# Sums of x in eight small pieces with buffers of their own, a ring for weights alone, and the last values placed behind the last scan step

## The chip, the cores and the metric

One core of a Trainium2 chip runs the whole kernel. The metric is device time in microseconds (us), the median over runs of the same program; lower is better. The engines are TensorE (PE: matmuls and transposes; PEld is its weight load), VectorE (DVE), ScalarE (ACT), GpSimd (POOL) and SyncE (SP), which here issues most of the DMAs in one queue.

## The reference

One layer of a hybrid encoder block on 1024 positions, with 16 learned meta tokens in front (T = 1040), d = 1024, all in float32. Cut to what matters:

```python
u = _rms_norm(h, pre_w)
z = u @ w_in                    # 1024 x 7680, one combined projection
rq, rk, rv, rg, aq, ak, av, ag, gr, ga = _split_in(z)

# branch A: retention, 4 heads, keys 128 wide, values 256 wide, chunks of 128,
# one scan forward and one backward, summed; then a norm per head
o_r = _bidirectional_retention(rq, rk, rv, lg_f, lg_b)[:, META_PAD:]
o_r = ((o_r - mu) * lax.rsqrt(var + EPS)).reshape(B, T, RET_V)
o_r = o_r * ret_nw * jax.nn.silu(rg)
y_r = o_r @ w_rb

# branch B: attention in a window of +-128, 8 heads in 2 groups, meta keys and a sink
o_a = _windowed_sink_attention(aq, ak, av, sink)[:, META_PAD:].reshape(B, T, ATT_Q)
y_a = (o_a * jax.nn.silu(ag)) @ w_ab

mix = jax.nn.sigmoid(gr) * y_r + jax.nn.sigmoid(ga) * y_a
return h + _rms_norm(mix @ w_o, post_w)
```

## The kernel before

**Matmuls.** A float32 product is made of three passes in a faster format (fp32r): each operand is split into a high part, cast by ScalarE or GpSimd, and a low part, which VectorE gets as the difference (the helper `dve_lo`, line 89). `mm3` then issues high by high, high by low and low by high, which are lines 73, 74 and 75 in the profile. In the names an `h` or `l` at the end tells the part: `wh` and `wl` are the halves of a weight tile `wr`, `weh` and `wel` those of `we`, `aqh` and `aql` those of `aq`, `kTh` and `kTl` those of the keys.

**Stages.** About 0 to 40 us: set-up, the norm, x transposed and kept in SBUF (`big`). To 343 us: the four retention heads, one after the other; each head's last work is a backward scan over the chunks (`pb` is the matmul with the scan's state), the head's norm (line 610), and `finish`, which transposes the results on TensorE (`to`, line 578), scales them on ScalarE into `ost`, and stores these to DRAM (`oTr_d`, line 586). Between these steps stand the projections that come next, the last of them `gen_av`: the attention's values in nine pieces (`pav`), the last two of which are held back by a scheduling mark until the transposes of the last head are issued (`follow(last["to"])`). From 350 to 600 us: attention. After 600 us: the gates, the two branch projections and the output projection, in which products of half matrices are combined so that seven are needed for eight (a phase with `bz`, and so on); TensorE hardly pauses there.

**Attention.** It runs over 32 chunks (four pairs of heads by eight blocks of queries). For each chunk `stage1` makes scores (`ps`), VectorE masks them into `raw` with the maximum, ScalarE takes the exponential (`p`) and its sum (`den`), GpSimd divides; `stage2` transposes `p` (`pt`) and splits it (`pah`, `pal`, `pm`, `pbh`, `pbl`); `stage3` multiplies with the values (`po`) and every second chunk stores the result `oa` to `oTa_d`. At the stage's start, the first column of `raw` is written by a copy (line 1332), and `split_q` makes the first queries `aqh` and `aql`.

**Fillers.** Between the stages of a chunk, `fill` runs steps of a list of other work, 200 in all, so that TensorE has matmuls while the softmax is under way: `gen_aq` (queries of the next heads, `paq`, 16 steps for each half), `gen_ak` (keys, `pak`), and `pre`: products for the gates' phase that can be made early (`pe`), in units 7 to 13 of half-matrix sums, stored to DRAM (`e`). The table `BEGUN` hangs other work on the numbers of these steps: at step s, before its matmuls, the listed jobs are issued. The jobs are the load of a unit's weights (`pre_fetch`, into `we`), the sums of these weights and their split (`pre_sums`, `pre_parts`), the load of the queries' weights (`fetch_aq`, into `wr`) and their split, a half at a time (`half_w`: `wh` and `wl`), the split of queries (`split_q`), the keys (`keys`: `kTh`, `kTl`), and the sums of x, below. A simulation of the engines at build time then sets the order of the instructions on each engine, within what the marks of `follow` demand; every engine runs its row in that order, and SyncE's queue starts its DMAs in order too.

**Sums of x.** The gates' phase needs differences of the quarters of x. `sum_fetch(k)` loads two tiles of 128x1024, `sum_row(k, part)` scales them on ScalarE and forms two of the four differences T1 to T4 on VectorE (128x512 each) and stores them to DRAM (`xs_d`); `get_sum` reads them back after 600 us. The tiles stand in the same ring as the weights:

```python
            t = keep.tile([P, 4, 256], F32, tag="wr", bufs=2, name=f"xs{i}{k}")
```

This ring, `wr`, has two tiles of 512 KB, and everything that is loaded in the attention stage goes through it: the weights `wr` of queries and keys, the weights `we` of the units, and the tiles `xs`. A load into a tile starts when all readers of what stood there are done, stores included. `x_to_out` copies the rows of x, 3 MB, from DRAM to the output in DRAM, to which the result is added later; it is issued after chunk 17 of attention.

Of the kernel before, what the change touches and what calls it, by code (L numbers as in the profile page):

```python
# [7 lines left out]
F32 = mybir.dt.float32  # L8
# [6 lines left out]
NM = 16  # L15
T = NM + SEQ
# [22 lines left out]
def block_kernel(ctx: ExitStack, tc: tile.TileContext, xT, x, w_in, w_rb, w_ab, w_out, vecs, dec, sink,  # L39
# [22 lines left out]


    e_d = {(u, p): dram.tile([P, 512], F32, tag=f"e{u}{p}", name=f"e{u}_{p}") for u in PRE for p in PRE[u]}
    xs_d = {n: dram.tile([4, P, 512], F32, tag=f"xs{n}", name=f"xs{n}") for n in ("T1", "T2", "T3", "T4")}
    pre_d = {n: [dram.tile([P, 4, 512], F32, tag=f"pre{n}{s}", name=f"pre{n}{s}") for s in range(2)]
             for n in ("T1", "T2", "T3", "T4")}

# [386 lines left out]
    def retention(h, fill):  # L455
# [118 lines left out]
        def finish(c):  # L574
            o = op[c - 1]
            to = p1(f"to{h}_{c}")
            for e_ in range(2):
                last["to"] = nc.tensor.transpose(to[:, P * e_:P * e_ + P], o[:, P * e_:P * e_ + P], ident).ins
            if c % 2 == 0:
                ost[0] = rp.tile([P, 2, 256], F32, tag="ost", bufs=2, name=f"ost{h}_{c}")  # L580
            w0 = P * ((c - 1) % 2)
            for e_ in range(2):
                nc.scalar.activation(ost[0][:, e_, w0:w0 + P], to[:, P * e_:P * e_ + P], AF.Copy,
                                     scale=rnw[:, 2 * h + e_:2 * h + e_ + 1])
            if c % 2 == 1:
                nc.sync.dma_start(
                    oTr_d[2 * h:2 * h + 2, :, P * (c - 1):P * (c + 1)].rearrange("e p t -> p e t"), ost[0])

        for c in range(NB, 0, -1):
            o = op[c - 1]  # L590
            if c > 1:
                nxt = kvb[c - 1]
                if c < NB:
                    nxt = rp.tile([P, 256], F32, tag="S", bufs=2, name=f"Sb{h}_{c}")
                    nc.vector.scalar_tensor_tensor(nxt, state["b"], cdb(h), kvb[c - 1], op0=ALU.mult, op1=ALU.add)
                state["b"] = nxt
                state["bs", c - 1] = split_state(nxt, f"b{h}_{c}")
            if c < NB:
                bh, bl = state["bs", c]
                pb = p3(f"pb{h}_{c}")  # L600
                mm3(pb[:, 0:256], qs(qh, c), qs(ql, c), bh, bl, True, True)
                nc.vector.scalar_tensor_tensor(o, pb[:, 0:256], qdb(h, c), o, op0=ALU.mult, op1=ALU.add)
            bs = rp.tile([P, 6], F32, tag="bs", bufs=2, name=f"bs{h}_{c}")
            mv = rp.tile([P, 2], F32, tag="mv", bufs=2, name=f"mv{h}_{c}")
            rs = rp.tile([P, 1], F32, tag="rs", bufs=2, name=f"rs{h}_{c}")
            nc.vector.bn_stats(bs, o)
            nc.vector.bn_aggr(mv, bs)
            near = nc.vector.tensor_scalar(rs, mv[:, 1:2], EPS, None, op0=ALU.add).ins
            nc.gpsimd.tensor_tensor(rs, rs, mhalf[:, 0:1], ALU.pow)
            state["n", c] = lambda o=o, mv=mv, rs=rs: nc.vector.tensor_scalar(o, o, mv[:, 0:1], rs, op0=ALU.subtract,  # L610
                                                                              op1=ALU.mult)
# [99 lines left out]
    SUMS = ("T1", (0, 0), (0, 1), (0, 0)), ("T3", (0, 1), (1, 1), (0, 1)), ("T2", (1, 1), (1, 1), (0, 0)), (  # L711
        "T4", (1, 0), (1, 0), (1, 1))

    def sum_fetch(k):

        for i in range(2):
            t = keep.tile([P, 4, 256], F32, tag="wr", bufs=2, name=f"xs{i}{k}").rearrange("p a b -> p (a b)")
            nc.sync.dma_start(t, xT[4 * i + k, :, NM:T])
            xsum[i] = t

    def sum_row(k, part):

        x = {}
        for i, t in xsum.items():
            if not part:
                nc.scalar.activation(t, t, AF.Copy, scale=vec[:, 4 * i + k:4 * i + k + 1])
            for j in range(2):
                x[i, j] = t[:, 512 * j:512 * j + 512]
        for n, o, a, b in SUMS[2 * part:2 * part + 2]:
            nc.vector.tensor_tensor(x[o], x[a], x[b], ALU.subtract)  # L730
# [569 lines left out]
    def attention():  # L1300
# [84 lines left out]
        def stage3(hp, n):  # L1385
# [12 lines left out]
            if n % 2:  # L1398
# [3 lines left out]


        chunks = [(hp, n) for hp in range(4) for n in range(NB)]
        fill = filler([hooked([gen_aq(0, 1), pieces(pre, 8), gen_aq(1, 0), gen_aq(1, 1), pieces(pre, 8), gen_aq(2, 0),
                               gen_ak(1, (0, 1)), gen_aq(2, 1), gen_ak(1, (2, 3)), gen_aq(3, 0), gen_aq(3, 1), pre], BEGUN)])[0]
        av = gen_av()
        next(av)
        with follow(last["to"]):
            next(av, None)  # L1410
        with follow(*latest):
            stage1(0, 0)
        for k, (hp, n) in enumerate(chunks):
# [29 lines left out]
    BEGUN = {0: [(pre_fetch, 7)], 4: [(pre_sums, 7)], 6: [(pre_parts, 7)], 8: [(fetch_aq, 1)],
             12: [(split_q, 0, 0, 1)], 16: [(half_w, 'q', 1, 0)], 19: [(half_w, 'q', 1, 1)],
             20: [(split_q, 0, 1, 1)], 21: [(sum_fetch, 0)], 30: [(sum_row, 0, 0)], 33: [(sum_row, 0, 1)],
             34: [(pre_fetch, 8)], 36: [(split_q, 1, 0, 0)], 41: [(pre_sums, 8)], 44: [(split_q, 1, 1, 0)],
             45: [(pre_parts, 8)], 46: [(fetch_aq, 2)], 52: [(split_q, 1, 0, 1)], 55: [(half_w, 'q', 2, 0)],
             58: [(half_w, 'q', 2, 1)], 60: [(split_q, 1, 1, 1)], 61: [(fetch_ak,)], 70: [(half_w, 'k', 1, 0)],
             73: [(half_w, 'k', 1, 1)], 75: [(sum_fetch, 1)], 76: [(split_q, 2, 0, 0)], 82: [(sum_row, 1, 0)],
             84: [(split_q, 2, 1, 0)], 86: [(sum_row, 1, 1)], 88: [(sum_fetch, 2)], 95: [(sum_row, 2, 0)],  # L1450
             98: [(sum_row, 2, 1)], 100: [(keys, 1, 1), (sum_fetch, 3)], 108: [(sum_row, 3, 0), (split_q, 2, 0, 1)],
             111: [(sum_row, 3, 1)], 113: [(fetch_aq, 3)], 116: [(split_q, 2, 1, 1)], 121: [(half_w, 'q', 3, 0)],
             122: [(keys, 1, 2)], 125: [(half_w, 'q', 3, 1)], 131: [(keys, 1, 3)], 138: [(pre_fetch, 9)],
             140: [(split_q, 3, 0, 0)], 145: [(pre_sums, 9)], 148: [(split_q, 3, 1, 0)], 150: [(pre_parts, 9)],
             151: [(pre_fetch, 10)], 156: [(split_q, 3, 0, 1)], 157: [(pre_sums, 10)], 160: [(pre_parts, 10)],
             161: [(pre_fetch, 11)], 164: [(split_q, 3, 1, 1)], 167: [(pre_sums, 11)], 169: [(pre_parts, 11)],
             171: [(pre_fetch, 12)], 175: [(pre_sums, 12)], 177: [(pre_parts, 12)], 179: [(pre_fetch, 13)],
             184: [(pre_sums, 13)], 187: [(pre_parts, 13)]}
# [110 lines left out]
```

## Time and profile before

| what | value |
|---|---|
| median of 3 runs | 1109.9 us (1106.97 to 1111.24) |
| the profiled execution | 1105.16 us, span 1103.4 us, mean granted clock of TensorE 0.989 |
| TensorE busy | 1064.3 us, 96% of the span |
| VectorE busy | 879.3 us, 80% |
| ScalarE busy | 508.9 us, 46% |
| GpSimd busy | 202.9 us, 18% |
| loads of weights in the ring (`wr`) | 29 of 512 KB, median 3.7 us from issue to landing |
| loads of x for the sums (`xs`) | 8 of 512 KB, median 3.6 us |

The span is the time from the first to the last instruction of the profiled execution. A group's row gives line, engine, operation, what is written and what is read, the shape, the count, the busy time, the mean of one in ns, and the idle time of the engine before it with what ended most of that. A row of the timeline gives the start, the duration, the instruction, and in brackets how long its engine had been idle and for whom.

### The profile page before, as it was taken

To read this page: it belongs to the slowest core of one execution; us is meant where nothing else is said; L and a number is where in the kernel's file an instruction comes from. 1 tells how busy PE (TensorE), PEld (TensorE's weight loads), DVE (VectorE), ACT (ScalarE), POOL (GpSimd) and SP (SyncE) were. 2 spreads that over 40 slices of the span, in tenths; PEclk is the share of its full clock that TensorE was granted. 3 is DMA by queue.
4 is the path that set the end of the run, shared out by engine and by line. 5 is a ranking of instruction groups with operands and counts; after the bars stand their busy time and mean duration, and the time that the engine had idled before them with its cause. 6 is when DMAs were issued, how large, how long until landed. Compare 5 with 4: busy or idle time off the path is not lost.

```text
span 1103.4 us, 17177 instructions
## 1 busy us (share of the span) xinstructions
PE 1064.3 (96%) x5939; PEld 917.9 (83%) x5939; DVE 879.3 (80%) x1789; ACT 508.9 (46%) x1118; POOL 202.9 (18%) x268
## 2 busy tenths in 40 slices
PE   8999999999999898987999999999999999999997
PEld 6898999988988787976888788878888888787886
DVE  7897778868976667785866989898979889877765
ACT  7241432513423545663466744545547545433442
POOL 3334224143332222331210000000000000010032
PEclk9999999999999998998999999999999999999999
DMA  7121102122121223364146877899963764789463
GB/s 285 39 68 58 58 20 68 58 76 76 41 77 58 87 90 111 115 208 146 58 163 200 302 244 240 309 335 346 363 217 109 244 210 169 233 196 334 146 115 77
DMA packets 82903, 175.18 MB, mean 159 GB/s; under 512 B 8784, under 2 KB 22608, under 8 KB 82000
## 3 DMA queue, kind: packets, MB, share of 16 engines
q1 hardware_dynamic: 78928, 167.51, 44.4%
q0 software_dynamic: 3456, 6.29, 3.8%
q8 instruction: 47, 0.77, 0.3%
q14 instruction: 40, 0.33, 0.1%
q10 hardware_dynamic: 432, 0.28, 0.1%
HBM read 119.52 MB, written 57.67 MB: 161 GB/s over the span
## 4 chain that ended last, share of the span: by engine, by line
PE 75%; DVE 11%; DMA 8%; issue 3%; ACT 2%; POOL 1%; SPq 0%; DVEq 0%; POOLq 0%; ACTq 0%
PE bz L73 6%; PE bz L74 6%; PE bz L75 6%; PE pv L73 3%; PE pv L74 2%; PE pv L75 2%; PE br L74 2%; PE br L73 2%; PE br L75 2%; PE bo L74 2%; PE bo L73 2%; PE bo L75 2%; PE ba L74 2%; PE ba L73 2%; PE ba L75 2%
## 5 line engine op out<-in xcount | busy, mean ns | idle before, releaser
L1194 POOL DMA_DIRECT2D mx_d<-c1a x4 | 3.7, 919 | 401.3 <-DVE c1a L1185 401.3
L75 PE MATMUL bz<-T,lhz 128*128 128x512 f32 x192 | 75.8, 395 | 0.0
L74 PE MATMUL bz<-T,llz 128*128 128x512 f32 x192 | 75.7, 394 | 0.0
L73 PE MATMUL bz<-T,lhz 128*128 128x512 f32 x192 | 75.2, 394 | 0.0
L73 PE MATMUL pv<-wh,big 128*128 128x256 f32 x256 | 73.2, 286 | 1.2 <-DVE m_qk L185 1.2
L74 PE MATMUL pv<-wh,big 128*128 128x256 f32 x256 | 73.0, 285 | 0.0
L75 PE MATMUL pv<-wl,big 128*128 128x256 f32 x256 | 72.7, 284 | 0.0
L74 PE MATMUL bz<-big,llz 128*128 128x512 f32 x176 | 69.7, 396 | 0.0
L73 PE MATMUL bz<-big,lhz 128*128 128x512 f32 x176 | 69.0, 396 | 0.5 <-ACT lhz L894 0.5
L75 PE MATMUL bz<-big,lhz 128*128 128x512 f32 x176 | 69.3, 394 | 0.0
L1347 POOL TENSOR_SCALAR p<-p,den 128x400 f32<-128x400 f32 (+1 forms) x60 | 35.4, 605 | 118.7 <-DVE den L1340 105.8
L73 PE MATMUL paq<-big,wh 128*128 128x512 f32 x128 | 53.4, 417 | 3.7 <-ACT wh L114 3.7
L1337 ACT ACTIVATE p<-raw,nm 128x401 f32<-128x401 f32 (+1 forms) x64 | 38.5, 602 | 36.9 <-DVE nm L1334 35.4
L74 PE MATMUL paq<-big,wl 128*128 128x512 f32 x128 | 52.2, 408 | 0.8 <-DVE wl L89 0.8
L1334 DVE CUSTOM_DVE_ANT_0 raw<-ps,mask,nsink 128x400 f32<-128x400 f32 (+1 forms) x64 | 36.8, 598 | 19.0 <-PE ps L75 18.7
L75 PE MATMUL paq<-big,wh 128*128 128x512 f32 x128 | 51.9, 406 | 0.0
L73 PEld LDWEIGHTS pv<-wh,big 128*128 128x128 f32 x256 | 48.2, 188 | 1.7 <-DVE m_qk L185 1.5
L74 PEld LDWEIGHTS pv<-wh,big 128*128 128x128 f32 x256 | 48.2, 188 | 0.2
L75 PEld LDWEIGHTS pv<-wl,big 128*128 128x128 f32 x256 | 48.3, 189 | 0.0
L74 PEld LDWEIGHTS bz<-T,llz 128*128 128x128 f32 x192 | 36.2, 188 | 8.4
L73 PEld LDWEIGHTS bz<-T,lhz 128*128 128x128 f32 x192 | 36.2, 188 | 8.4
L75 PEld LDWEIGHTS bz<-T,lhz 128*128 128x128 f32 x192 | 36.2, 188 | 8.4
(630 smaller groups left out, 3626.5 us busy)
## 6 DMA issues: line engine op xcount, KB each, us to landing
wrz<-in_w_in_dram SPq DMA_DIRECT2D x32, 512.0 KB, 5.8
wr<-in_w_in_dram SPq DMA_DIRECT2D x29, 512.0 KB, 3.7
e<-e SPq DMA_DIRECT2D x40, 256.0 KB, 3.6
we<-in_w_in_dram SPq DMA_DIRECT2D x16, 512.0 KB, 3.6
tg<-tg_d SPq DMA_DIRECT2D x32, 256.0 KB, 5.0
T<-preT SPq DMA_DIRECT2D x6, 1024.0 KB, 7.2
oTr_d<-ost SPq DMA_DIRECT2D x16, 256.0 KB, 2.1
xs<-in_xT_dram SPq DMA_DIRECT2D x8, 512.0 KB, 3.6
```

Source lines behind the costliest of these rows:

```text
L73: nc.tensor.matmul(o, ah, bh, start=first, stop=False, **kw)
L74: nc.tensor.matmul(o, al, bh, start=False, stop=False, **kw)
L75: latest[:] = [nc.tensor.matmul(o, ah, bl, start=False, stop=last, **kw).ins]
L1194: nc.gpsimd.dma_start(d, to, accum_op=ALU.add)
L1334: nc.vector.tensor_tensor_reduce(raw[e_][:, 1:1 + wid], s[:, 0:wid], mask[:, mo:mo + wid], -SCALE, nsink[:, hd:hd + 1], ALU.add, ALU.min, ...
L1337: last["exp"] = nc.scalar.activation(p[:, 0:1 + wid], raw[e_][:, 0:1 + wid], AF.Exp, scale=-1.0, bias=nm_[:, e_:e_ + 1], accum_out=den[:, ...
L1347: nc.gpsimd.tensor_scalar(pt[e_][:, 0:wid], pt[e_][:, 0:wid], den[:, e_:e_ + 1], 1.0, op0=ALU.mult, op1=ALU.mult)
```

## The change

It has four parts.

1. The sums of x are made in eight pieces (`q`, each a half of the columns of one `k`) instead of four pairs, in two buffers of their own (tag `xs`, 256 KB each). A piece is two loads of 256 KB, two scalings on ScalarE of 128x512, four differences on VectorE of 128x256, made in place, and two stores of 256 KB. In all there are 16 loads for 8, 16 scalings of half the size for 8, 32 differences of half the size for 16, and 16 stores as before.
2. The ring `wr` holds weights alone, and `BEGUN` has other step numbers. Loads are asked for at steps further ahead of their use, the fetch for the queries of heads 2 and 3 (`fetch_aq(1)`) stands at step 0, and unit 7 comes behind the first half of these queries (in `hooked`, `gen_aq(1, 0)` goes before `pieces(pre, 8)`).
3. The two last pieces of the values follow the last scan step's matmul (`last["pb"]`) and no longer the last head's transposes (`last["to"]`).
4. `x_to_out` is issued in three parts, after chunks 12, 17 and 21.

```diff
-    xs_d = {n: dram.tile([4, P, 512], F32, tag=f"xs{n}", name=f"xs{n}") for n in ("T1", "T2", "T3", "T4")}
+    xs_d = [dram.tile([4, P, 2, 512], F32, tag=f"xs{i}", name=f"xs{i}") for i in range(2)]
...
-                last["to"] = nc.tensor.transpose(to[:, P * e_:P * e_ + P], o[:, P * e_:P * e_ + P], ident).ins
+                nc.tensor.transpose(to[:, P * e_:P * e_ + P], o[:, P * e_:P * e_ + P], ident)
...
-                mm3(pb[:, 0:256], qs(qh, c), qs(ql, c), bh, bl, True, True)
+                last["pb"] = mm3(pb[:, 0:256], qs(qh, c), qs(ql, c), bh, bl, True, True)
...
-    def sum_fetch(k):
+    def sum_fetch(q):
+        k, c = q // 2, slice(256 * (q % 2), 256 * (q % 2) + 256)
         for i in range(2):
-            t = keep.tile([P, 4, 256], F32, tag="wr", bufs=2, name=f"xs{i}{k}").rearrange("p a b -> p (a b)")
-            nc.sync.dma_start(t, xT[4 * i + k, :, NM:T])
-            xsum[i] = t
+            xsum[i] = t = ap.tile([P, 2, 256], F32, tag="xs", bufs=2, name=f"xs{i}{q}")
+            nc.sync.dma_start(t, xT[4 * i + k, :, NM:T].rearrange("p (j t) -> p j t", j=2)[:, :, c])
 
-    def sum_row(k, part):
+    def sum_row(q):
+        k, c = q // 2, slice(256 * (q % 2), 256 * (q % 2) + 256)
         x = {}
         for i, t in xsum.items():
-            if not part:
-                nc.scalar.activation(t, t, AF.Copy, scale=vec[:, 4 * i + k:4 * i + k + 1])
+            nc.scalar.activation(t, t, AF.Copy, scale=vec[:, 4 * i + k:4 * i + k + 1])
             for j in range(2):
-                x[i, j] = t[:, 512 * j:512 * j + 512]
-        for n, o, a, b in SUMS[2 * part:2 * part + 2]:
+                x[i, j] = t[:, j]
+        for _, o, a, b in SUMS:
             nc.vector.tensor_tensor(x[o], x[a], x[b], ALU.subtract)
-            nc.sync.dma_start(xs_d[n][k], x[o])
+        for i, t in xsum.items():
+            nc.sync.dma_start(xs_d[i][k][:, :, c], t)
...
-        fill = filler([hooked([gen_aq(0, 1), pieces(pre, 8), gen_aq(1, 0), gen_aq(1, 1), pieces(pre, 8), gen_aq(2, 0),
+        fill = filler([hooked([gen_aq(0, 1), gen_aq(1, 0), pieces(pre, 8), gen_aq(1, 1), pieces(pre, 8), gen_aq(2, 0),
...
-        with follow(last["to"]):
+        with follow(last["pb"]):
             next(av, None)
...
-            if k == 17:
-                x_to_out()
+            if k in (12, 17, 21):
+                x_to_out({12: 0, 17: 4, 21: 6}[k])
...
-    BEGUN = {0: [(pre_fetch, 7)], 4: [(pre_sums, 7)], 6: [(pre_parts, 7)], 8: [(fetch_aq, 1)],
-             12: [(split_q, 0, 0, 1)], 16: [(half_w, 'q', 1, 0)], 19: [(half_w, 'q', 1, 1)],
...
-             111: [(sum_row, 3, 1)], 113: [(fetch_aq, 3)], 116: [(split_q, 2, 1, 1)], 121: [(half_w, 'q', 3, 0)],
+    BEGUN = {0: [(fetch_aq, 1)], 9: [(half_w, 'q', 1, 0)], 12: [(half_w, 'q', 1, 1)],
+             13: [(split_q, 0, 0, 1), (pre_fetch, 7)], 14: [(sum_fetch, 0)], 18: [(split_q, 0, 1, 1)],
...
```

Beside the rows shown, the load of the weights for the queries of the last two heads (`fetch_aq(3)`) goes from step 113 to 106 and its casts from 121 and 125 to 115 and 119; the load of unit 11 goes from 161 to 153 and its split (`pre_parts(11)`) from 169 to 164.

Where the last head's transposes stand on TensorE, at the end of retention and ahead of attention, the row before reads (`pb` is the last scan step, `to` the transposes of finished chunks, `pav` a value piece):

```order
L75 MATMUL pb_1_4639<-Slb_2_4573,qh_0_3613 128x256
L578 MATMUL to_3_4684<-ident,op_2_3638 128x128 x2
L578 MATMUL to_2_4691<-ident,op_1_3637 128x128 x2
L578 MATMUL to_1_4697<-ident,op_0_3636 128x128 x2
L73 MATMUL pav_4916<-wh_0_4723,big_0_111 128x256
L74 MATMUL pav_4916<-wh_0_4723,big_1_113 128x256
```

And the changed kernel at the same place, the pieces of values shortened, up to the first scores:

```order
L75 MATMUL pb_1_4637<-Slb_2_4571,qh_0_3611 128x256
L73 MATMUL pav_4914<-wh_0_4721,big_0_109 128x256
...
L578 MATMUL to_3_4682<-ident,op_2_3636 128x128 x2
...
L578 MATMUL to_2_4689<-ident,op_1_3635 128x128 x2
...
L578 MATMUL to_1_4695<-ident,op_0_3634 128x128 x2
L73 MATMUL pav_4941<-wh_1_4725,big_0_110 128x256
...
L73 MATMUL ps_0_4974<-kTh_4311,aqh_00_4970 128x272
L73 MATMUL ps_0_4987<-kTh_4311,aqh_01_4983 128x272
L74 MATMUL ps_0_4974<-kTh_4311,aql_00_4971 128x272
```

The first matmul of the values comes right behind the scan step, the transposes stand among the 48 matmuls of the two pieces, and six of these follow the last transpose ahead of the scores.

The same place on VectorE, before and then after: `op` is the head's norm, `val` the low parts of a value piece, `raw` the copy of the sink, `aql` the low part of the first queries.

```order
L610 TENSOR_SCALAR op_0_3636<-op_0_3636,mv_1_4645,rs_1_4646 128x256
L1279 MEMSET pm_4714 128x256
L1279 MEMSET pm_4715 128x256
L1332 COPY raw_4980<-nsink 128x1
L1332 COPY raw_4993<-nsink 128x1
L89 TENSOR_TENSOR aql_00_4973<-aq_00_4626,aqh_00_4972 128x512
L89 TENSOR_TENSOR aql_01_4986<-aq_01_4677,aqh_01_4985 128x512
L1295 SCALAR_TENSOR_TENSOR val_4713<-pav_4916,rcol,vah 128x256
```

```order
L610 TENSOR_SCALAR op_0_3634<-op_0_3634,mv_1_4643,rs_1_4644 128x256
L1297 SCALAR_TENSOR_TENSOR val_4711<-pav_4914,rcol,vah 128x256
L1297 SCALAR_TENSOR_TENSOR val_4711<-pav_4941,rcol,vah 128x256
L1281 MEMSET pm_4712 128x256
L1281 MEMSET pm_4713 128x256
L1334 COPY raw_4978<-nsink 128x1
L1334 COPY raw_4991<-nsink 128x1
L89 TENSOR_TENSOR aql_00_4971<-aq_00_4624,aqh_00_4970 128x512
```

Both `val` now stand ahead of the copies into `raw`, and these still stand ahead of `aql`.

On SyncE, in the first chunks of attention, the row before (with the numbers in the names: `we8` are the weights of unit 8, `e7` products of unit 7, `xs00` and `xs10` the two tiles of x, `xsT1` to `xsT4` its sums):

```order
L718 DMA xs00_5243<-in_xT_dram 128x1024
L1399 DMA oTa_d_67<-oa0_0_5166 128x2x256
L718 DMA xs10_5245<-in_xT_dram 128x1024
L801 DMA e7_3_77<-e7_3_5306 128x512
L731 DMA xsT1_90<-xs00_5243 128x512
L1399 DMA oTa_d_67<-oa0_2_5339 128x2x256
L731 DMA xsT3_92<-xs00_5243 128x512
L731 DMA xsT2_91<-xs10_5245 128x512
L761 DMA we8_1_5415<-in_w_in_dram 128x1024
L731 DMA xsT4_93<-xs10_5245 128x512
L761 DMA we8_0_5414<-in_w_in_dram 128x1024
```

And after, from the first load of x on:

```order
L719 DMA xs00_5147<-in_xT_dram 128x2x256
L719 DMA xs10_5149<-in_xT_dram 128x2x256
L762 DMA we7_1_5141<-in_w_in_dram 128x1024
L762 DMA we7_0_5140<-in_w_in_dram 128x1024
L1401 DMA oTa_d_67<-oa0_0_5169 128x2x256
L762 DMA we8_1_5326<-in_w_in_dram 128x1024
L762 DMA we8_0_5325<-in_w_in_dram 128x1024
L732 DMA xs0_90<-xs00_5147 256x1x256
L719 DMA xs01_5398<-in_xT_dram 128x2x256
L732 DMA xs1_91<-xs10_5149 256x1x256
L719 DMA xs11_5400<-in_xT_dram 128x2x256
```

The weights of unit 8 stood among the stores of the first sums; now those of units 7 and 8 both stand ahead of the first store, and the next load of x stands between the two stores of the piece before.

On ScalarE, where the keys of the second group are made (`akr` are the rotated keys, `wh` a half of the last queries' weights), before and then after:

```order
L1380 CAST pbh_1_6547<-pt_2_1_6535 128x256
L114 CAST wh_0_6554<-wr_0_6417 128x1024
L692 CAST kTh_6255<-akr_2_6490 128x256
L1337 ACTIVATE p_3_6598,den_3_6593<-raw_6342,nm_3_6592 128x401
L1337 ACTIVATE p_3_6605,den_3_6593<-raw_6351,nm_3_6592 128x401
```

```order
L1382 CAST pbh_1_6574<-pt_2_1_6562 128x256
L692 CAST kTh_6276<-akr_2_6513 128x256
L726 ACTIVATE xs_6416<-xs_6416,vec 128x512
L726 ACTIVATE xs_6418<-xs_6418,vec 128x512
L1339 ACTIVATE p_3_6627,den_3_6622<-raw_6371,nm_3_6621 128x401
```

The cast of the weights no longer stands between `pbh` and the keys; a scaling of x has come behind them.

More of the change, by code (lines that the diff above doesn't have):

```diff
@@ L1047, in get_sum @@
             t = stage(f"x{n}{k}", n in ("T2", "T3"))
-            nc.sync.dma_start(t, xs_d[n][k])
+            i, j = next(o for m, o, *_ in SUMS if m == n)
+            nc.sync.dma_start(t, xs_d[i][k][:, j])
             split_b(n, k, t)
@@ L1437, in attention @@
                 yield
-            if k == 17:
-                x_to_out()
+            if k in (12, 17, 21):
+                x_to_out({12: 0, 17: 4, 21: 6}[k])
         stage3(*chunks[-1])
-    BEGUN = {0: [(pre_fetch, 7)], 4: [(pre_sums, 7)], 6: [(pre_parts, 7)], 8: [(fetch_aq, 1)],
-             12: [(split_q, 0, 0, 1)], 16: [(half_w, 'q', 1, 0)], 19: [(half_w, 'q', 1, 1)],
[L1445 to L1451, printed above, removed]
-             111: [(sum_row, 3, 1)], 113: [(fetch_aq, 3)], 116: [(split_q, 2, 1, 1)], 121: [(half_w, 'q', 3, 0)],
[L1453 to L1458, printed above, removed]
@@ L1460, in x_to_out @@
-    def x_to_out():
+    BEGUN = {0: [(fetch_aq, 1)], 9: [(half_w, 'q', 1, 0)], 12: [(half_w, 'q', 1, 1)],
+             13: [(split_q, 0, 0, 1), (pre_fetch, 7)], 14: [(sum_fetch, 0)], 18: [(split_q, 0, 1, 1)],
+             22: [(pre_sums, 7)], 25: [(pre_parts, 7)], 26: [(sum_row, 0), (pre_fetch, 8)], 28: [(split_q, 1, 0, 0)],
+             30: [(sum_fetch, 1)], 35: [(split_q, 1, 1, 0)], 37: [(pre_sums, 8)], 40: [(pre_parts, 8)],
+             41: [(fetch_aq, 2)], 42: [(sum_row, 1)], 46: [(sum_fetch, 2)], 52: [(split_q, 1, 0, 1)],
+             54: [(half_w, 'q', 2, 0)], 58: [(half_w, 'q', 2, 1)], 60: [(split_q, 1, 1, 1)], 61: [(fetch_ak,)],
+             63: [(sum_row, 2)], 66: [(sum_fetch, 3)], 70: [(half_w, 'k', 1, 0)], 73: [(half_w, 'k', 1, 1)],
+             76: [(split_q, 2, 0, 0)], 79: [(sum_row, 3)], 82: [(sum_fetch, 4)], 84: [(split_q, 2, 1, 0)],
+             93: [(sum_row, 4)], 95: [(sum_fetch, 5)], 100: [(keys, 1, 1)], 106: [(sum_row, 5), (fetch_aq, 3)],
+             108: [(split_q, 2, 0, 1)], 109: [(sum_fetch, 6)], 115: [(half_w, 'q', 3, 0)], 116: [(split_q, 2, 1, 1)],
+             119: [(half_w, 'q', 3, 1)], 122: [(keys, 1, 2)], 124: [(sum_row, 6)], 126: [(pre_fetch, 9)],
+             128: [(sum_fetch, 7)], 131: [(keys, 1, 3)], 136: [(pre_sums, 9)], 139: [(pre_parts, 9)],
+             140: [(pre_fetch, 10), (split_q, 3, 0, 0)], 143: [(sum_row, 7)], 148: [(split_q, 3, 1, 0)],
+             149: [(pre_sums, 10)], 152: [(pre_parts, 10)], 153: [(pre_fetch, 11)], 156: [(split_q, 3, 0, 1)],
+             161: [(pre_sums, 11)], 164: [(pre_parts, 11), (split_q, 3, 1, 1)], 165: [(pre_fetch, 12)],
+             172: [(pre_sums, 12)], 174: [(pre_parts, 12)], 175: [(pre_fetch, 13)], 182: [(pre_sums, 13)],
+             184: [(pre_parts, 13)]}
@@ L1462, in x_to_out @@
+    def x_to_out(r):
         with tc.issue_after(stored[-1]):
-            for r in (0, 4, 6):
-                nc.sync.dma_start(out[P * r:P * r + 2 * P], x[P * r:P * r + 2 * P])
+            nc.sync.dma_start(out[P * r:P * r + 2 * P], x[P * r:P * r + 2 * P])
     del wak[:]
```

## The prediction

> **What bounds the kernel now.** I read the page's busy times first, then the stretches of 50 us, then TensorE's rows in order of time for every idle gap, and last the chain and the rows of the engine that each gap waited for.
>
> ```profile
> PE 1064.3 (96%) x5939; PEld 917.9 (83%) x5939; DVE 879.3 (80%) x1789; ACT 508.9 (46%) x1118; POOL 202.9 (18%) x268
> ```
>
> TensorE is the bound, before and behind the places below: what it wins there the end wins. Only its 39 idle us and its slow clock can be won. The stretches (PE, PEld, DVE, ACT, POOL busy; granted clock; DMA share) say where:
>
> ```profile
> 350.00:400.00 50.00, 46.73 (x244) 39.35 (x244) 32.98 (x72) 26.45 (x64) 11.57 (x16) 0.97 0.21 74
> 400.00:450.00 50.00, 45.71 (x244) 39.41 (x243) 34.52 (x69) 24.03 (x58) 12.07 (x16) 0.93 0.35 107
> 450.00:500.00 50.00, 45.11 (x308) 40.98 (x307) 41.31 (x98) 31.03 (x78) 15.79 (x20) 1.00 0.57 192
> 500.00:550.00 50.00, 45.53 (x250) 39.62 (x248) 32.84 (x74) 22.16 (x59) 12.48 (x17) 0.93 0.26 87
> 550.00:600.00 50.00, 48.45 (x271) 41.95 (x269) 32.87 (x74) 32.63 (x81) 5.89 (x10) 0.97 0.47 157
> ```
>
> These are the attention stage, idle for 18.5 us, and the clock sinks there. TensorE's gaps from 340 to 600 us (start, duration, and in brackets the idle time and its releaser):
>
> ```profile
> 342.79 0.41 PE L578 MATMUL to<-ident,op 128*128 128x128 f32 x2 [1.90 <-DVE op L610]
> 343.64 0.41 PE L578 MATMUL to<-ident,op 128*128 128x128 f32 x2 [0.45 <-DVE op L610]
> 361.82 0.63 PE L1357 MATMUL pt<-ident,p 128*128 128x128 f32 x4 [2.14 <-DVE pal L89]
> 380.50 0.45 PE L74 MATMUL ps<-kTh,aql 128*128 128x400 f32 x1 [0.90 <-DVE aql L89]
> 416.88 0.59 PE L74 MATMUL ps<-kTh,aql 128*128 128x272 f32 x1 [3.98 <-DVE aql L89]
> 479.05 0.38 PE L1360 MATMUL pt<-ident,p 128*16 128x128 f32 x2 [1.59 <-DVE raw L1332]
> 497.68 0.45 PE L73 MATMUL ps<-kTh,aqh 128*128 128x400 f32 x1 [2.54 <-ACT kTh L692]
> 508.93 0.50 PE L73 MATMUL paq<-big,wh 128*128 128x512 f32 x1 [3.71 <-ACT wh L114]
> 510.19 0.79 PE L74 MATMUL paq<-big,wl 128*128 128x512 f32 x1 [0.76 <-DVE wl L89]
> 566.56 0.50 PE L73 MATMUL pe<-big,weh 128*128 128x512 f32 x1 [0.79 <-ACT weh L780]
> 567.82 0.66 PE L74 MATMUL pe<-big,wel 128*128 128x512 f32 x1 [0.76 <-DVE wel L89]
> ```
>
> Around them the granted clock (the third number from the end):
>
> ```profile
> 342.00:346.00 4.00, 2.77 (x22) 2.59 (x23) 1.56 (x6) 2.28 (x6) 0.58 (x1) 1.00 0.29 97
> 358.00:366.00 8.00, 5.86 (x29) 4.80 (x28) 6.50 (x13) 3.73 (x11) 2.44 (x3) 0.82 0.22 80
> 410.00:421.00 11.00, 6.71 (x31) 5.54 (x30) 9.81 (x20) 5.44 (x13) 2.22 (x3) 0.70 0.30 80
> 496.00:503.00 7.00, 5.03 (x21) 4.21 (x22) 4.38 (x11) 4.04 (x10) 0.55 (x1) 0.77 0.88 311
> 504.00:513.00 9.00, 4.53 (x18) 3.46 (x17) 2.29 (x4) 1.72 (x3) 0.33 (x1) 0.83 0.42 148
> 564.00:571.00 7.00, 5.45 (x22) 4.29 (x21) 3.46 (x7) 3.21 (x8) 1.18 (x2) 0.78 0.59 181
> ```
>
> A gap of 1.90 us left the clock at 1.00; one of 2.14 cost (1 - 0.82) x 8 = 1.4 us more in slow matmuls. So a gap above about two us is priced with 1.2 to 1.6 us on top. [...]
>
> **What the gaps wait for.** The chain (start, us) ahead of the gaps at 416.88, 508.93 and 567.82, and VectorE ahead of 361.82:
>
> ```profile
> 402.34 4.23 DMA xsT<-xs
> 406.63 3.58 DMA we<-in_w_in_dram
> 490.69 5.58 DMA xsT<-xs
> 496.33 11.47 DMA wr<-in_w_in_dram
> 557.32 4.30 DMA we<-in_w_in_dram
> 357.72 1.23 DVE L89 TENSOR_TENSOR wel<-we,weh 128x1024 fp32r<-128x1024 f32 x1 [1.11 <-ACT weh L780]
> ```
>
> Twice a weight waits until a sum of x has left the shared ring; once it is asked for too late.
>
> **The change, part by part.**
>
> 1. Ring for weights alone, earlier loads. Gap 416.88: idle 3.98; half speed lasted (1 - 0.70) x 11 x 2 = 6.6 us, 3.7 of it idle anyway, so 2.9 x 0.5 = 1.5 of clock: 5.5 us. Its fetch no longer waits for a store of xs and is asked for 11 steps ahead of its sums (250 us for 200 steps: 1.25 us a step, so 14 us) where a landing takes 3.7: all 5.5 goes. Gap 508.93: 3.71 + 0.76, and by the same working (0.17 x 9 x 2 - 0.76) / 2 = 1.15 of clock: 5.6, goes: the load is asked for at hook 106, its casts at 115 and 119 for matmuls from step 128, and the ring is empty since 73. Gap 566.56: 0.79 + 0.76 + 1.15, 2.7, goes: pre_parts(11) moves from hook 169 to 164, its fetch from 161 to 153.
>
> ```profile
> wr<-in_w_in_dram SPq DMA_DIRECT2D x29, 512.0 KB, 3.7
> ```
>
> 2. Unit 7 behind gen_aq(1, 0). Gap 361.82 (2.14 + 1.4 = 3.6) was pal behind the sums of unit 7 and wel; now nothing stands there: 3.6. In their place the splits of the query weights come a chunk earlier than at 380.50; aql no longer stands behind them: of 0.9 I take 0.6.
>
> 3. Sums in pieces. VectorE pays 32 subtracts of 128x256 for 16 of 128x512:
>
> ```profile
> L730 DVE TENSOR_TENSOR xs<-xs 128x512 f32<-128x512 f32 x8 | 6.1, 763 | 0.7 <-ACT xs L726 0.6
> L730 DVE TENSOR_TENSOR xs<-xs,xs 128x512 f32<-128x512 f32 x8 | 5.5, 690 | 1.6 <-ACT xs L726 1.5
> L89 DVE TENSOR_TENSOR kTl<-akr,kTh 128x256 fp32r<-128x256 f32 x4 | 1.7, 416 | 0.0
> ```
>
> 32 x 0.416 = 13.3 against 11.6: 1.7 us more, beside matmuls, on an engine that is busy 174.5 of 250 us here. Without that cover it would be 1.7 us. ScalarE's 16 halves for 8 wholes and eight more DMA issues on SP lie beside it too; what SP's row could cost is rival E. The full rows that stood close together around 479 us (VectorE 41.31 of 50) go apart: of the 1.59 there I take 1.5. [...]
>
> 4. Gap 497.68 mostly stays. kTh stood behind one cast of 1.05 us that now goes ahead, but two wl of 1.23 us now stand in VectorE's row before the same values: of 2.54 and 0.23 x 7 = 1.6 of clock, 4.1, I take 0.4.
>
> 5. The last values behind pb, not to. This takes the 2.35 us at 342.79 away and, I think, pays more:
>
> ```profile
> 340.39 0.28 PE L75 MATMUL pb<-Slb,qh 128*128 128x256 f32 x1
> 343.81 0.36 PE L73 MATMUL pav<-wh,big 128*128 128x256 f32 x1
> 344.09 0.63 ACT L583 ACTIVATE ost<-to,rnw 128x128 f32<-128x128 f32 x2 [0.18 <-PE to L578]
> 346.98 0.21 DVE L1332 COPY raw<-nsink 128x1 f32<-128x1 f32 x2 [2.94 <-DMA oTr_d<-ost]
> 347.11 1.29 DVE L89 TENSOR_TENSOR aql<-aq,aqh 128x512 fp32r<-128x512 f32 x2
> 349.58 0.29 PE L73 MATMUL ps<-kTh,aqh 128*128 128x272 f32 x1
> ```
>
> The copy into raw waits for the last store of ost, and aql stands behind it. Before, 5.8 us of pav (343.81 to 349.58) hid that. Now pav runs from 340.51 with the transposes inside, and would end at 340.51 + 5.77 + 0.75 = 347.0; but the last transpose stands six matmuls before that end, at 346.1, and from it to the copy took 346.98 - 343.64 = 3.3: raw at 349.4, the first aql done 0.13 + 0.65 later, near 350.2. The score matmul that takes it came right behind 349.58; now it comes at 350.3: 0.7 later, with a hole of some 3.0 us that costs about 1.5 of clock: 2.2 lost. Bounds: 2.6 won if the store is not awaited, 4.2 lost if it takes the 4.1 us of the slowest ost store instead of 2.1; I take the working, since its rows are this very place.
>
> ```profile
> DMA to landing us min/median/max: 2.1/2.1/4.1
> ```
>
> [...]
>
> 6. x to out in three parts: it lay over the wr of 11.47 us; its gain is in the gap at 508.93.
>
> Sum: 5.5 + 5.6 + 2.7 + 3.6 + 0.6 + 1.5 + 0.4 - 2.2 = 17.7. New short waits in VectorE's crowded chunks: between 0 and the 4.1 of the dearest one that no weight's load caused; I take 2.1, the middle, for want of a nearer row. Gain 15.6. The profiled execution took 1105.16 us (span 1103.4), 4.7 below the median of 1109.9; 1105.16 - 15.6 = 1089.6, and on the median 1094.3: 1094.
>
> **Rivals.**
>
> A. As above, 1094, own range 1089 to 1099: 0.62.
>
> B. Everything goes, the hole at the stage's start too: 18.5 idle, 2.35, and clock of 1.4 + 1.5 + 1.6 + 1.15 + 1.15 = 6.8: 27.7, so 1082 to 1088. Against it: the copy's wait at 346.98. 0.16.
>
> C. The loads still land late, with other waits before them: unit 7's fetch must wait for the second wl of the queries' weights and by that lands only some 3 us before its sums, an estimate from the rows' order. Two holes of 5.6 back: 1094 + 11 = 1105; range 1099 to 1106. 0.12.
>
> D. The ring was not the cause; its fetches were hidden anyway. Then parts 2 to 5 are left, 3.6 + 0.6 + 1.5 + 0.4 - 2.2 - 2.1 = 1.8: 1108. Against it: the chain's rows. 0.06.
>
> E. Slower: SP's one queue. The 16 fetches and 16 stores of xs stand among the weights' loads; a store waits for VectorE, the next fetch for that store to land (the xsT rows above: 4.23 and 5.58). If that holds five of the weights' loads beyond their lead, five holes of 5.6 come: 1094 + 28 = 1122. It decides once a load is held over 6 us: the shortest lead, eight steps of 1.25, less the landing of 3.7. 0.04.
>
> A change of 0.5%, 5.5 us, is about what a measurement tells from none. Faster: A, B and most of C, 0.87; same: D and the rest of C, 0.09; slower: 0.04. Range 1083 to 1104: it leaves out D, E and a little of B and C.
>
> **What the next profile would show.** Right: no gap of TensorE released by wh, wl or weh over 1 us, VectorE never idle for a DMA of we, clock 1.00 from 400 to 490; a hole of about 3 us ahead of the first aql with the copy into raw released by oTr_d; ps for kTh still over 1.5 us. Wrong: the first score matmuls before 349 us, or a chain through xs stores into we or wr.

## The result: 1090.2 us, 1.6% faster, and the profile after

The changed kernel takes 1090.24 us in the median of 4 runs (1089.63 to 1091.47), the kernel before, beside it, 1108.43; the ratio is 0.9836, 95% interval 0.9808 to 0.9863. The forecast was 1094. The profiled execution went from 1105.16 to 1089.63 us, 15.5 less, where the sum of the prediction had 15.6. In the medians the gain is 18.2 us, 2.6 more than the sum: the profiled execution of the kernel before lies below all four of its timed runs (1106.24 to 1111.24). So the close agreement of the profiles is in part luck, and it hides terms that were wrong in both directions.

The busy times, from the page of the changed kernel, and its attention stage in stretches of 50 us:

```profile
PE 1060.5 (97%) x5939; PEld 915.7 (84%) x5939; DVE 880.7 (81%) x1805; ACT 510.3 (47%) x1126; POOL 201.8 (19%) x268
```

```profile
350.00:400.00 50.00, 48.50 (x250) 40.94 (x251) 35.63 (x80) 26.96 (x67) 13.89 (x18) 0.97 0.25 81
400.00:450.00 50.00, 50.00 (x299) 44.26 (x299) 38.70 (x86) 29.79 (x73) 11.77 (x16) 1.00 0.44 138
450.00:500.00 50.00, 44.80 (x281) 40.49 (x281) 38.38 (x97) 28.77 (x78) 14.86 (x20) 0.93 0.49 158
500.00:550.00 50.00, 49.50 (x289) 43.20 (x287) 42.53 (x91) 28.51 (x74) 13.37 (x18) 1.00 0.42 136
550.00:600.00 50.00, 50.00 (x277) 43.01 (x276) 36.66 (x75) 35.25 (x82) 3.53 (x6) 1.00 0.60 192
```

TensorE's idle time here fell from 18.5 to 7.2 us. Two stretches have none. What is left stands mostly at two places, and there the clock is still below 1.00. These are all of TensorE's gaps above 0.3 us from 340 to 600 us:

```profile
347.75 0.91 PE L73 MATMUL ps<-kTh,aqh 128*128 128x272 f32 x2 [1.07 <-ACT aqh L646]
349.84 0.39 PE L74 MATMUL ps<-kTh,aql 128*128 128x272 f32 x1 [1.19 <-DVE aql L89]
362.53 0.63 PE L1359 MATMUL pt<-ident,p 128*128 128x128 f32 x4 [1.24 <-DVE pal L89]
481.57 0.83 PE L1359 MATMUL pt<-ident,p 128*128 128x128 f32 x4 [0.70 <-DVE pal L89]
490.10 0.70 PE L73 MATMUL ps<-kTh,aqh 128*128 128x400 f32 x1 [4.31 <-ACT kTh L692]
```

No row waits for `wh`, `wl`, `weh` or `wel` any more. The wait for `kTh` grew from 2.54 to 4.31 us.

Where the 15.6 us of span (1103.4 to 1087.8) came from is read from the starts of the same value products (`po`) in both timelines:

| stretch, by its last `po` before / after | gained | forecast |
|---|---|---|
| start to 369.87 / 369.00 (0.40 of it before 253 us) | 0.9 | 3.6 - 2.2 = 1.4 |
| to 410.47 / 408.91 | 0.7 | 0.6 |
| to 424.76 / 416.38 | 6.8 | 5.5 |
| to 483.43 / 473.37 | 1.7 | 1.5 |
| to 511.21 / 498.40 | 2.7 | 5.6 + 0.4 = 6.0 |
| to 560.03 / 547.23 | 0.0 | -2.1 (new short waits) |
| to 576.57 / 560.13 | 3.6 | 2.7 |
| to the end, 1103.4 / 1087.8 | -0.8 | 0 |

### The profile page after: what moved, and what is told of

The parts are those of the page before. It is cut to its first block, busy times and chain, and to the rows that moved or that the text cites. A ratio compares the mean times of both kernels' runs of the same rounds, so it can differ in the third digit from the quotient of the medians.

```text
span 1087.8 us, 17211 instructions
## 1 busy us (share of the span) xinstructions
PE 1060.5 (97%) x5939; PEld 915.7 (84%) x5939; DVE 880.7 (81%) x1805; ACT 510.3 (47%) x1126; POOL 201.8 (19%) x268
## 4 chain that ended last, share of the span: by engine, by line
PE 85%; DVE 6%; DMA 3%; issue 2%; ACT 2%; POOL 1%; SPq 0%; DVEq 0%; ACTq 0%; POOLq 0%
PE bz L73 8%; PE bz L74 8%; PE bz L75 8%; PE pv L73 3%; PE pv L74 2%; PE pv L75 2%; PE br L74 2%; PE br L73 2%; PE br L75 2%; PE bo L74 2%; PE bo L73 2%; PE bo L75 2%; PE ba L74 2%; PE ba L73 2%; PE ba L75 2%
```

## The experiments

Each was timed in five rounds against the kernel before, runs on one chip within a group of kernels. The changed kernel run once more gave 1089.27 us (1088.22 to 1091.14); its nine runs together have a median of 1089.7. The runs of one variant spread over 1.4 to 4 us, those of the kernel before, 9 to 11 in a group, over 3.3 to 9.2 us.

**Part 1 alone.** The kernel before with the sums in pieces and in their own buffers, at the changed kernel's steps for the sums; all else as before.

```diff
-            t = keep.tile([P, 4, 256], F32, tag="wr", bufs=2, name=f"xs{i}{k}").rearrange("p a b -> p (a b)")
+            xsum[i] = t = ap.tile([P, 2, 256], F32, tag="xs", bufs=2, name=f"xs{i}{q}")
...
+    BEGUN: sum_fetch(q), sum_row(q) at 14, 26; 30, 42; 46, 63; ... ; weights at their old steps
```

> The kernel before with part 1 alone: the sums of x in eight pieces in buffers of their own, at the steps of the changed kernel; the weights' loads at their old steps, unit 7 first, the values behind to, x to out in one go. Theory ring (sharing the ring held the weights): the gap at 416.88 us (3.98 idle and its slow clock) goes and the gaps at 361.82, 508.93 and 566.56 stay, since their loads are asked for as late as before: 5.5 to 7 us, so 1101 to 1103 us. Rival lead (the loads were only asked for too late): the gap at 416.88 stays, 1107 to 1109 us.

1091.62 us (1091.2 to 1092.58), ratio 0.9852, interval 0.983 to 0.9873: 16.1 us of the gain, against the 6 that were expected. TensorE's gaps in its timeline:

```profile
342.60 0.58 PE L578 MATMUL to<-ident,op 128*128 128x128 f32 x2 [1.90 <-DVE op L610]
362.80 0.74 PE L1359 MATMUL pt<-ident,p 128*128 128x128 f32 x4 [2.14 <-DVE pal L89]
381.49 0.45 PE L74 MATMUL ps<-kTh,aql 128*128 128x400 f32 x1 [0.90 <-DVE aql L89]
414.88 0.39 PE L74 MATMUL ps<-kTh,aql 128*128 128x272 f32 x1 [1.56 <-DVE aql L89]
492.24 0.45 PE L73 MATMUL ps<-kTh,aqh 128*128 128x400 f32 x1 [3.16 <-ACT kTh L692]
554.47 0.50 PE L73 MATMUL pe<-big,weh 128*128 128x512 f32 x1 [0.73 <-ACT weh L781]
555.74 0.50 PE L74 MATMUL pe<-big,wel 128*128 128x512 f32 x1 [0.76 <-DVE wel L89]
```

The gap at 416.88, which was to go, shrank to 1.56 with no loss of clock (1.00 from 412 to 422 us). The one at 508.93, which was to stay, went as well, with the load at its old step 113 and the copy of x in one go. The rows of this load say why (engine, operation, count, durations in ns, first and last start), of the kernel before and then of this one:

```profile
L105 SPq DMA_DIRECT2D wr<-in_w_in_dram x28: 327/330/382, 15.0 to 496.3; - x28
```

```profile
L105 SPq DMA_DIRECT2D wr<-in_w_in_dram x28: 327/332/418, 14.8 to 446.2; - x28
```

The last `wr` was issued at 496.3 us only because a sum of x sat in its tile; with the tile free it goes out at 446.2, some 47 us ahead of its cast. So both of the large gaps go without an earlier step of the load. This run changes buffers, pieces and the steps of the sums together; the next one takes the buffers alone back. The gaps at 361.82 (2.14) and 566.56 (0.73 + 0.76) stayed, as expected of loads that are asked for late.

**The ring shared again.** The changed kernel, with the pieces of x in the weights' ring, and four of the eight sums moved by one to three steps.

```diff
-            xsum[i] = t = ap.tile([P, 2, 256], F32, tag="xs", bufs=2, name=f"xs{i}{q}")
+            t = keep.tile([P, 4, 256], F32, tag="wr", bufs=2, name=f"xs{i}{q}")
+            xsum[i] = t = t[:, 0:2]
```

> The changed kernel with the eight pieces of x put back into the weights' ring, at the new steps (the arithmetic of a piece a few steps earlier where a weight's load would otherwise come between). Theory ring: the waits of weights for stores of xs come back, one to three holes of 4 to 5 us with their clock, 1096 to 1104 us. Rival lead: the loads are early enough to bear the sharing, 1090 to 1092 us.

1098.25 us (1095.37 to 1099.38), ratio 0.9908 (0.9887 to 0.993): some 8 us of the gain are lost. The chain ahead of 454 us, where one of the new gaps stands, runs from a store of x into a load of weights, as it did before the change:

```profile
433.38 2.44 DMA xs<-xs
435.83 3.79 DMA wr<-in_w_in_dram
```

The theory of the ring holds in both directions, but the holes are smaller than expected, the largest of the new ones 1.51 us: with the early loads, sharing costs some 8 us. Why it is not the 16 that part 1 alone gained is not shown; the earlier loads are the likely reason.

**Part 3 undone.** The changed kernel with `follow(last["to"])`.

```diff
-        with follow(last["pb"]):
+        with follow(last["to"]):
```

> The changed kernel with the last two value pieces held until the last transposes again (part 3 undone). Theory of the prediction (part 3 costs 2.2 us here, since the pieces covered the last store): 1088 us, the hole ahead of the first aql is gone and 2.3 us of waits ahead of the transposes are back. Rival (the two are a wash, since the hole of the changed kernel is 2.26 us and the old waits were 2.35): 1089.5 to 1091 us. Second rival (part 3 is a gain): 1092 us or more.

1087.64 us (1085.87 to 1089.57), ratio 0.9816 (0.9792 to 0.9839), about 2 us below the changed kernel. The rows at the border are the old ones, 1.90 and 0.45, and its clock from 350 to 400 us is 1.00:

```profile
350.00:400.00 50.00, 48.34 (x264) 41.09 (x263) 36.15 (x82) 27.63 (x69) 13.88 (x18) 1.00 0.25 80
```

Idle time is a wash, 2.35 against 2.26. What differs at the border is the clock, 1.00 here and 0.97 in the changed kernel; this run had its own slow stretch earlier, from 34 to 42 us (0.79). From the last matmul `pb` to the first `po` takes, in all the profiles that bear on this (slow stretches are the time at half speed there):

| kernels | slow stretch | `pb` to first `po`, us |
|---|---|---|
| part 3 undone (this run; in the better kernel below) | none | 27.01; 27.03 |
| parts 1 and 2 alone, below | 3.4 us | 28.22 |
| part 3 kept, `raw` as it was (four kernels) | 3.4 us | 28.70 to 29.17 |
| part 3 kept, `raw` as it was (two profiles) | 6.8 us | 29.71; 29.98 |
| part 3 kept, `raw` moved, below (two kernels) | 3.4 us | 27.75; 27.90 |

So with the same slow stretch part 3 costs 0.5 to 1.0 us, and 1.8 us in the mean of six profiles against three, since all six pay for a slow stretch and only one of the three does.

**Raw and xs swapped in memory.** The changed kernel, so that the first copy into `raw` lies over no `ost`.

```diff
-                    raw[e_] = aw.tile([P, 401], F32, tag=f"raw{e_}", bufs=1, name=f"raw{hd}")
+                    raw[e_] = ap.tile([P, 401], F32, tag=f"raw{e_}", bufs=1, name=f"raw{hd}")
-            xsum[i] = t = ap.tile([P, 2, 256], F32, tag="xs", bufs=2, name=f"xs{i}{q}")
+            xsum[i] = t = aw.tile([P, 2, 256], F32, tag="xs", bufs=2, name=f"xs{i}{q}")
```

> The changed kernel with the two tiles raw and the two tiles xs swapped in memory, so that the first copy into raw lies where no ost was and waits for no store. Theory of the prediction (that store holds the first aql): aql comes 1.2 us earlier, the hole ahead of the scores shrinks from 2.26 to about 1.1 us and the clock stays at 1.00 behind it, 1087 to 1088.5 us. Rival (something else holds aql, the values' casts on ScalarE or the second aql's own memory): the hole stays at 2 us and the time at 1090.

1088.27 us (1085.96 to 1089.37), ratio 0.9818 (0.9791 to 0.9845). First the copy in the changed kernel, then the gaps of this one at the border:

```profile
348.98 0.21 DVE L1334 COPY raw<-nsink 128x1 f32<-128x1 f32 x2 [0.72 <-DMA oTr_d<-ost]
```

```profile
348.10 0.91 PE L73 MATMUL ps<-kTh,aqh 128*128 128x272 f32 x2 [1.07 <-ACT aqh L646]
349.33 0.39 PE L74 MATMUL ps<-kTh,aql 128*128 128x272 f32 x1 [0.32 <-DVE aql L89]
```

The wait for `aql` fell from 1.19 to 0.32: the store held it. The clock did not stay at 1.00, though (0.79 from 349 to 357 us), and the 1.4 us between 1088.27 and the changed kernel's 1089.7 are within the spread of the runs. The mechanism is shown; its price is 0.8 to 1.4 us by the table above, with the same slow stretch.

**x to out in one go.** The changed kernel with all three copies after chunk 17.

```diff
-            if k in (12, 17, 21):
-                x_to_out({12: 0, 17: 4, 21: 6}[k])
+            if k == 17:
+                for r_ in (0, 4, 6):
+                    x_to_out(r_)
```

> The changed kernel with the 3 MB of x copied to the output in one go after chunk 17 again. Theory (the loads lead by enough): the landing of the next wr goes from about 4 back to about 11 us, and still no gap of TensorE waits for it, 1090 to 1091 us. Rival (the copy is what made wr late): a hole ahead of paq released by wh or wl, 1093 to 1096 us.

1088.13 us (1086.19 to 1090.23), ratio 0.9819 (0.9796 to 0.9843). No gap waits for weights, but the time lies below the 1090 to 1091 us that were expected, and the next run says how much of the 1.6 us is scatter. Nor could the load land late: the last `wr` goes out at 444.0 us here, the copy of x only at 485.9. So this run does not test what the copy costs a load that it meets.

**Parts 1 and 2 alone.** Part 3 undone and x to out in one go, in one kernel.

> The changed kernel without parts 3 and 4: sums in their own buffers and the new steps for the weights, values behind to, x to out in one go. If part 3 costs 2.6 us and part 4 brings nothing, as the two runs with one of them undone read, then 1086 to 1088 us; against the 1091.6 us of part 1 alone this is what part 2 is worth, 4 to 5 us (the gaps at 361.82 and 566.56, 3.6 and 2.7 by the prediction's sum, less new waits). Rival (part 2 is worth nothing, since the ring alone was the cause): 1090 to 1092 us.

1087.59 us (1085.68 to 1088.65), ratio 0.9812 (0.9785 to 0.9839). Beside part 3 undone, 1087.64, this says that part 4 is worth nothing. Beside x to out in one go, 1088.13, it says that part 3 costs 0.5 us; part 3 undone beside the changed kernel says 2.1. Between these the times do not decide; the table above has 1.8 in the mean. Against part 1 alone, 1091.62, part 2 is worth 4.0 us. So of the gain part 1 made some 16, part 2 some 4, and parts 3 and 4 gave up to 2 back.

**The keys earlier.** The changed kernel with the third piece of keys ahead of a half of the queries.

```diff
-                               gen_ak(1, (0, 1)), gen_aq(2, 1), gen_ak(1, (2, 3)), gen_aq(3, 0), ...
+                               gen_ak(1, (0, 1, 2)), gen_aq(2, 1), gen_ak(1, (3,)), gen_aq(3, 0), ...
     BEGUN:
-    108: split_q(2, 0, 1)   116: split_q(2, 1, 1)   122: keys(1, 2)
+    106: keys(1, 2)   113: split_q(2, 0, 1)   122: split_q(2, 1, 1)
```

> The changed kernel with the third piece of keys made ahead of the queries of the same pair of heads (steps 96 to 103 instead of 112 to 119), its cast at step 106. Theory (the scores at 490 us wait for keys whose cast stands behind a chunk's softmax, which two casts' low parts hold up): the gap of 4.31 us and its 6.8 us of half clock go, and the queries' piece, now later, is still in time: 4.3 + 1.3 = 5 to 6 us less, 1084 to 1086 us. Rival (VectorE is the bound there, full in this stretch, so the wait only changes its name): another gap of 2 to 4 us within 20 us, 1088 to 1091 us.

1085.88 us (1085.42 to 1087.06), ratio 0.9799 (0.9773 to 0.9825). The wait for `kTh` is gone, and the clock from 450 to 500 us is 1.00:

```profile
486.84 0.45 PE L73 MATMUL ps<-kTh,aqh 128*128 128x400 f32 x1 [0.46 <-DVE nm L1336]
489.56 0.83 PE L1359 MATMUL pt<-ident,p 128*128 128x128 f32 x4 [1.34 <-DVE pal L89]
490.86 0.38 PE L1362 MATMUL pt<-ident,p 128*16 128x128 f32 x2 [0.48 <-DVE pbl L89]
```

The rival has a part in it: 2.28 us of new waits for VectorE stand within 4 us of the old place. The gain is 3.4 us against the changed kernel beside it, less than the 5 to 6 that were expected.

**The casts of the last weights later.** The changed kernel with `half_w('q', 3, ...)` at 121 and 125 for 115 and 119.

> The changed kernel with the two casts of the last queries' weights back at their old steps, 121 and 125 instead of 115 and 119, the load as early as in the changed kernel. Theory (the two wl that now stand ahead of the scores' masks on VectorE, 2 x 1.23 us, made the gap before kTh grow from 2.54 to 4.31): it falls back to 2.5 to 3.2 us, 1 to 2 us less, 1088 to 1089 us. Rival (the keys' own rotation is what is late): the gap stays at 4.3, 1089.5 to 1090.5.

1090.05 us (1088.36 to 1091.99), ratio 0.9839 (0.9824 to 0.9854). The gap fell to 3.57 us, less than expected, and the time not at all. Its chain now holds no `wl`, but a cast on ScalarE, `wh`, that the later steps have put between `pbh` and `kTh`:

```profile
486.17 0.48 ACT pah L1370
...
488.11 1.05 ACT wh L114
489.16 0.32 ACT kTh L692
489.47 0.04 issue
489.52 0.70 PE ps L73
```

Without `wl`, `pbh` starts at 487.84 and no longer at 489.37, 1.5 us earlier, and the 1.05 us of this cast take most of that back. So the theory of `wl` holds as far as `pbh`. The rival does not hold: GpSimd was done with the keys' rotation at 484.67, well ahead of `kTh`.

**Two better kernels.** The keys earlier, with parts 3 and 4 undone:

> The piece of keys early, and parts 3 and 4 undone. If the runs' differences add up (5 us for the keys, 0.5 to 2.6 for part 3, none for part 4): 1082.5 to 1085 us. Rival (without the hole of 4.3 us ahead the waits meet at VectorE): 1085.5 to 1087 us.

1083.96 us (1082.66 to 1084.81), ratio 0.9782 (0.9769 to 0.9796). And the keys earlier, raw and xs swapped, part 3 kept, x to out in one go:

> The piece of keys early, raw and xs swapped in memory, x to out in one go, and part 3 kept: the values cover nothing at the border, but the first aql waits for no store. If the differences add up: 1083.5 to 1085.5 us; and against the run with part 3 undone the border costs about the same (1.4 us of hole here, 2.35 us of waits there), so the two lie within 1 us of each other unless one of them pays a step of the clock there more often.

1082.58 us (1082.17 to 1084.51), ratio 0.9774 (0.9761 to 0.9787), the fastest of all, 0.9 us below its expected range; the two lie 1.4 us apart, within their spread. Against the changed kernel's 1089.7 they take 5.7 and 7.1 us less.

## Why the prediction was right, and which of its steps were not

**Item 1, the ring.** Right in its sign and almost in its size: the stretch around 416.88 gave 6.8 us for 5.5, the one around 566.56 gave 3.6 for 2.7. The clock's share of the first was too small: the slow stretch lasted from 414.4 to 421.2 us, at a granted clock of 0.50, so 2.5 us of it were idle and not 3.7, and it cost 2.2 us, not 1.5. The reason that it gave for the gap at 508.93, an earlier load, was not needed, and neither was item 6: part 1 alone took that gap away with the load at its old step and the copy in one go, and part 4 changed nothing that the runs can tell. The 11.47 us of `wr` were real, but the load went out late for want of a tile, and so behind the copy. Whether an earlier load or the parted copy alone would also have closed this gap, with the ring shared, was not run.

**Item 2, unit 7.** The first stretch gave 0.5 us behind 253 us, where this term and the border were to give 1.4. The wait for `pal` did not go, it changed its cause: 2.14 became 1.24. The item said that nothing stands ahead of `pal` now, and left out what is next in VectorE's row, the rotation of the queries that came forward in place of unit 7. The chain of the changed kernel shows it (start, us, what):

```profile
360.27 0.39 DVE m_aq L184
360.65 0.31 issue
360.97 0.70 DVE m_aq L185
361.69 0.69 DVE pal L89
```

**Item 3, the pieces.** Right: 32 differences took 0.42 us each, 13.5 in all for 13.3 forecast, beside matmuls.

```profile
L730 DVE TENSOR_TENSOR xs<-xs x16: 405/420/427, 387.1 to 520.5; 128x256 f32<-128x256 f32 x16
L730 DVE TENSOR_TENSOR xs<-xs,xs x16: 416/422/426, 388.6 to 520.0; 128x256 f32<-128x256 f32 x16
```

Rival E, a queue held by stores of x, did not come: no gap of TensorE waits for a weight.

**Item 4, the keys.** This is the term that was mis-sized. It saw two `wl` ahead in VectorE's row, and still took 0.4 us of gain; the wait grew by 1.77 us, and half speed behind it lasted 6.8 us (0.69 from 486 to 497 us) instead of 3.4 (0.66 from 499 to 504 us in the kernel before). The chain behind the gap at 490.10:

```profile
483.22 0.15 DVE wl L89
483.38 0.99 issue
484.37 1.23 DVE aql L89
485.60 0.03 issue
485.63 0.64 DVE raw L1336
...
489.37 0.03 ACT pbh L1382
...
489.64 0.42 ACT kTh L692
490.06 0.04 issue
490.10 0.70 PE ps L73
```

The scores' mask `raw` waits for one `wl` and for the queries' `aql`, of 1.23 us each (the second `wl` comes behind it, at 486.74), the softmax for `raw`, `pbh` for the softmax, and `kTh` stands behind `pbh` in ScalarE's row, although GpSimd was done with its keys at 485.05:

```profile
483.28 1.77 POOL L186 TENSOR_TENSOR akr<-m_ak,m_ak 128x256 f32<-128x256 f32 x1 [1.48 <-DVE m_ak L185]
```

The stretch to 498.40 gave 2.7 for 6.0. That the sum came out all the same is luck: the 2.1 us of new short waits, taken as a middle for want of a row, did not come where they were looked for, and the stretches around 416.88 and 566.56 gave 2.2 more than forecast. That made up for the 3.3 missing here, 0.5 in the first stretch and 0.8 behind 576 us, of which the runs show no cause.

**Item 5, the border.** Right in its mechanism, near in its size: the copy into `raw` was forecast for 349.4 and came at 348.98, released by `oTr_d` as said; the hole was 2.26 us for 3.0, and in two parts. The first of them, 1.07, waits for `aqh` on ScalarE and was not seen: two score matmuls need no `aql` and ran in the hole, from 347.75. So the forecast's own sign of being wrong, score matmuls before 349 us, came, although the copy held the first `aql` as it said. The price of 2.2 us, 0.7 of it delay and 1.5 clock, fits the runs: 0.5 to 1.0 us with the same slow stretch, 1.8 in the mean. The clock did fall behind the hole, to 0.79 from 349 to 357 us.

**The clock's price.** The step "a gap of 1.90 us left the clock at 1.00; one of 2.14 cost" read a threshold from two gaps, and the runs do not show one there. The same 1.90 us ahead of `to` cost nothing in the kernel before, and half speed for 3.4 us in part 1 alone (1 - 0.66, times 5 us, times 2); of the five profiles that have this hole, two paid. The prices of 1.2 to 1.6 us were also low, since the stretches that they were read from end inside the slow ones: that behind 361.82 lasted 3.4 us and not 2.9, so it cost 1.7.

```profile
342.00:347.00 5.00, 4.13 (x22) 3.79 (x23) 1.41 (x5) 2.27 (x6) 0.58 (x1) 0.66 0.40 119
```

## What to carry to other kernels

A buffer ring that is shared by two streams can make one wait for the other's stores (in the chain before, 4.23 us of a store of x ahead of a load of weights), and an earlier step for a load does not by itself bring the load forward (with the ring shared again the load at 435.83 us still stood behind a store of 2.44 us): look first at when the load was issued against the step that asked for it, and give the slow stream tiles of its own. When a wait's cause is moved out of an engine's row, part of the wait can stay under another name, as it did for `pal` and, with the keys earlier, for `kTh`; read what stands next in that row, and follow it as far as the engine that is the bound. And when a sum comes out right, compare it stretch by stretch before its terms are believed.

## What the runs showed of the hardware

From 340 to 600 us TensorE's granted clock falls at times to half speed (0.50 in the stretch from 365 to 366 us of the kernel before). That kernel has five such slow stretches there, within 363 to 367, 414 to 422, 499 to 504, 509 to 514 and 567 to 572 us; worked out from the mean clocks of these windows, 0.57, 0.57, 0.66, 0.66 and 0.66, the second is some 6.9 us long and the others some 3.4 each. Behind the hole at the border the changed kernel and its second run have (1 - 0.79) x 8 x 2 = 3.4 and (1 - 0.57) x 8 x 2 = 6.9 us of half speed, with nearly the same holes:

```profile
349.00:357.00 8.00, 7.07 (x24) 5.61 (x25) 3.89 (x14) 2.56 (x8) 2.14 (x4) 0.79 0.16 51
```

```profile
349.00:357.00 8.00, 6.63 (x18) 5.56 (x19) 4.05 (x14) 2.67 (x8) 2.08 (x4) 0.57 0.22 63
```

Behind the wait for `kTh`, 4.31 us in both, the changed kernel had (1 - 0.69) x 11 x 2 = 6.8 and the kernel with raw moved (1 - 0.84) x 11 x 2 = 3.5:

```profile
486.00:497.00 11.00, 6.90 (x26) 6.22 (x27) 8.25 (x23) 7.23 (x19) 1.94 (x3) 0.69 0.59 212
```

```profile
486.00:497.00 11.00, 7.57 (x33) 6.65 (x34) 8.40 (x22) 7.24 (x21) 3.13 (x5) 0.84 0.63 216
```

In the profiles read closely, a hole was followed by no slow stretch (1.90 us at 342.79 in the kernel before, clock 1.00), by one of some 3.4 us or by one of some 6.8; what decides between them the runs do not show. This is a likely part of the spread of one kernel's runs: in one group of eleven runs of the kernel before, the fastest (1102.29 us) had a mean granted clock of 0.992 and the slowest (1111.52) one of 0.985, which is 7.7 of the 9.2 us; in a group of nine on another chip, time and clock did not go together (1107.72 us at 0.986, 1112.44 at 0.987). So a hole of about two us is priced, as an estimate from these rows, as zero to 3.4 us of lost work (half of the 6.8 us at half speed) rather than with one number.
